# Attention values on one core: leading and trailing parts as one operand of 128 columns, two products per block, halves added by DVE

## The chip, the cores and the metric

The kernel runs on one core of a Trainium2 chip. The metric is the time of one execution in microseconds (us), the median over the runs shown. TensorE is called PE (PEld is its loading of the stationary operand), VectorE DVE, ScalarE ACT, GpSimd POOL, SyncE SP.

## The reference, cut to what matters

One transformer-like layer of 512 frames and 1024 channels: a projection, three mixers (a state space model, an attention, a spatial gating unit), a gated merge, a residual norm, a feed-forward block and a second residual norm, all in float32. The change touches the attention's last step alone. With 8 heads of 64 channels and blocks of 128 queries, it is

```
p = jax.nn.softmax(s, axis=-1).astype(v.dtype)
return jnp.einsum('bhqk,bkhd->bqhd', p, v)
```

where the mask keeps a key when its chunk of 64 frames is not later than the query's, so a block of 128 keys meets the queries from its own block on: 512, 384, 256 and 128 of them for the four key blocks.

## The kernel before

Every float32 operand x of a large product is split into a leading part (x rounded to the type fp32r, by ACT as a rule) and a trailing part (x minus the leading part, by DVE as a rule). A product is made of three: leading by leading, leading by trailing, trailing by leading. `mm3` (line 72) issues these three matmuls into one PSUM bank.

All engines' instructions are put in order when the kernel is built, by a planner (class at line 83, its loop `run` at line 380). Tasks are generators; each holds the next operation, or three matmuls as one group that is not parted. The planner knows a cost for each operation, takes the one that could start first by its own clock, and lets one of lower priority number pass if that would start nearly as soon. So the main stream (priority 5.0) is filled in wherever the attention (2.0) isn't ready; norm and weight tasks (0 to 0.5) go ahead of both, and the dot products of the modulation (`ada2`, 3.0) come behind the attention. On the chip each engine takes its instructions strictly in the planned order and waits on semaphores.

The main stream (`main`, line 1468) is, around the attention: `kept_gates(0)` (tiles `pz`, 24 matmuls each), then `branch(0, ...)` for the state space result (tiles `pp` out of `zs`, 12 matmuls each, eight tiles), then `branch(1, ...)` for the attention's result (tiles `pp` out of `ymla`, eight tiles of 12), the output projection (`po` out of `mT`) and the first norm (`norm1`, line 1847), whose transposed result feeds the feed-forward block. `branch(1, ...)` is planned only when the last head has been planned. Of its first tile, matmuls 10 to 12 are the first to read the last of the four `ymla` tiles.

The attention has one task per head (`head`, line 839). In order: the query product `pq`, scaled and split into `qh` (DVE, ACT, DVE); four score tiles `s`, each with DVE's fill and maximum, ACT's exponential, DVE's reciprocal and ACT's scaling into `pr`; the transposes `px` of `pr` on PE, evicted as leading and trailing parts `pb` (ACT, then DVE) of 512, 384, 256 and 128 columns; for each key block j three matmuls into `po`, with 64 columns of the value tile `vv` as the stationary operand and `pb` moving; ACT's copy of `po` into half the rows of `o`; after every second head the split of `o` into `ymla` (ACT, DVE). A head's transposes and values begin after the values of the head before are done (`o_done`), and its scores after the scores of the head before (`s_done`). PSUM has 8 banks: four are kept for the main stream, so the attention has at most four, three of which (`po` and two `px`) belong to a head's values.

The value tiles are made once, early, in `latents` (line 751): per block of 128 frames one product `pv` of 128x512, ACT's copy to the leading half of the tile, DVE's difference to the trailing half.

Of the kernel before, what the change touches and what calls it, by code (L numbers as in the profile page):

```python
# [14 lines left out]
AF = mybir.ActivationFunctionType  # L15
ALU = mybir.AluOpType
# [3 lines left out]
P = 128  # L20
# [3 lines left out]
NT = 4  # L24
# [43 lines left out]
def ts(i, n=P):  # L68
    return slice(i * n, (i + 1) * n)


def mm3(o, w, x, start, stop):

    T = PE[0]
    return [(T, "matmul", (o, w[0], x[0]), dict(start=start, stop=False)),
            (T, "matmul", (o, w[0], x[1]), dict(start=False, stop=False)),
            (T, "matmul", (o, w[1], x[0]), dict(start=False, stop=stop))]
# [5 lines left out]
class Planner:  # L83
# [27 lines left out]
    class Recorder:  # L111
# [8 lines left out]
        def drop(self, *tiles):  # L120
            self.ops.append((None, self.plan.drop, tiles, {}))
# [103 lines left out]
    def get(self, pool, cls, name, shape=None, dt=F32):  # L225
        yield lambda: self.pools[pool].room(cls)
        return self.take(pool, cls, name, shape, dt)

    def gets(self, pool, cls, *names):

        p = self.pools[pool]
        yield lambda: p.room(cls) if p.free_for(cls) >= len(names) else INF
        return [self.take(pool, cls, n) for n in names]
# [200 lines left out]
def hybrid_kernel(ctx: ExitStack, tc: tile.TileContext, a: dict, out: bass.AP):  # L434
# [6 lines left out]
    V, S, G, T, Y = pl.V, pl.S, pl.G, pl.T, pl.Y  # L441
    get, gets, take, drop, hold, when, spawn = pl.get, pl.gets, pl.take, pl.drop, pl.hold, pl.when, pl.spawn
# [8 lines left out]
    def f(ap):  # L451
        return ap.bitcast(F32)


    def sl(w, s):
        return w[0][:, s], w[1][:, s]
# [259 lines left out]
    L = {}  # L716
# [34 lines left out]
    def latents():  # L751
        r = pl.Recorder(pl)
# [16 lines left out]
        yield from r.run()  # L769
        kvn = L["kvn"]  # L770
        w = yield from wv.wait()
        L["vv"] = []
        for t in range(NT):
            o = yield from get("s4", "x", "vv", (P, 2, N), F32R)
            pv = yield from get("ps", "x", "pv")
            for c in range(2):
                r.mm3(pv, (kvn[c][:, 0, ts(t)], kvn[c][:, 1, ts(t)]), sl(w, ts(c, 512)), c == 0, c == 1)
            r.S.activation(o[:, 0, :], pv, AF.Copy)
            r.V.tensor_tensor(o[:, 1, :], pv, f(o[:, 0, :]), op=ALU.subtract)
            r.drop(pv)  # L780
            yield from r.run()
            L["vv"].append(o)
        wv.free()
        v_done.set()
        yield kv_go
# [7 lines left out]
        for hh in range(2):  # L793
            o = 64 * (1 - hh)
# [9 lines left out]
        for p in range(4):  # L804
# [6 lines left out]
            for e in range(2):  # L811
                q = slice(64 * e, 64 * e + 64)
# [3 lines left out]
            for e in range(2):  # L816
                q = slice(64 - 64 * e, 128 - 64 * e)
# [21 lines left out]
    def head(h):  # L839
        e = h % 2  # L840
        r = pl.Recorder(pl)
# [12 lines left out]
        pq = yield from get("ps", "x", "pq")  # L854
# [38 lines left out]
        for t in (3, 2, 0, 1):  # L893
            n = P * (t + 1)
# [14 lines left out]
        vv = L["vv"]  # L909
        if h > 0:  # L910
            yield o_done[h - 1]
        po, *pxs = yield from gets("ps", "x", "po", "px", "px")
        po = po[:64, :]

        turned = [Event() for _ in range(NT)]

# [19 lines left out]
        for j in range(NT):  # L936
            yield turned[j]
            n = N - P * j
            pb = pt[j, "b"]
            yield mm3(po[:, P * j:], (vv[j][:, 0, ts(h, 64)], vv[j][:, 1, ts(h, 64)]), (pb[:, 0, :n], pb[:, 1, :n]),  # L940
                      j == 0, j == NT - 1)
            drop(pb)
        drop(*(pt[t, "t"] for t in range(1, NT)))
        o = o32[h // 2]
        r.S.activation(o[64 * e:64 * e + 64, :], po, AF.Copy)
        r.drop(po)
        yield from r.run()
        o_done[h].set()
# [4 lines left out]
            yield from r.run()  # L953
        heads_left[0] -= 1
        if heads_left[0] == 0:
            drop(*vv)
            ymla_done.set()

    s_done = [Event() for _ in range(HEADS)]
# [508 lines left out]
    def main():  # L1468
# [17 lines left out]
        for m in range(4):  # L1486
            spawn(put_u(m), POST)
        spawn(latents(), LAT0)
        spawn(ada2(), ADA)
        for h in range(HEADS):  # L1490
            spawn(head(h), ATT + 0.01 * h)
# [491 lines left out]
```

## Time and profile before

| | us |
|---|---|
| median of 3 runs (lowest, highest) | 880.0 (879.49, 880.49) |
| the profiled execution's own time | 878.67 |
| its span | 876.9 |
| PE busy in the span | 852.6 |
| DVE busy | 593.8 |
| ACT busy | 365.0 |
| POOL busy | 88.7 |

The profile is of one execution; the span runs from its first instruction to its last. In the profile every operation carries line 97, the planner's helper, so groups are told apart by tile names. A matmul's own duration holds its passage through the array, which overlaps with the next one's; the distance from one start to the next is what a matmul costs in a stream. The chain of waits shows such costs, since it counts each piece up to the start of the next.

### The profile page before, as it was taken

Reading aid. Unit: us, or ns where it says so; the run is one execution under the profiler, and the core shown is the slowest. Engines: PE = TensorE matmul, PEld = TensorE weight load, DVE = VectorE, ACT = ScalarE, POOL = GpSimd, SP = SyncE. Lnnn points to the kernel's source line nnn. Section 1 sums busy time; section 2 is a strip of 40 time slices with the busy share of each in tenths; the row PEclk is TensorE's granted clock in tenths of the full one; section 3 lists DMA queues with packets and bytes.
Section 4 is the critical chain, followed back from the end, with each engine's and each line's share of the span. In section 5 each row is a group of like instructions: output and inputs, shape, how many; then the busy total and the mean of one; then the engine's idle time right before and its main releaser. Section 6 shows DMA issues by size and latency. Waiting matters only on the chain.

```text
span 876.9 us, 11401 instructions
## 1 busy us (share of the span) xinstructions
PE 852.6 (97%) x4258; PEld 710.0 (81%) x4258; DVE 593.8 (68%) x1161; ACT 365.0 (42%) x614; POOL 88.7 (10%) x98
## 2 busy tenths in 40 slices
PE   9999999999999989999999799999999999999995
PEld 8888888888888868888887699888888888888884
DVE  6989999999977579887859974634433334125436
ACT  3556554555446557675334543122222222211301
POOL 0003113202021000000002500000000000001025
PEclk9999999999999989999999999999999999999998
DMA  9972133434584344676730517322222222322401
GB/s 340 405 264 74 49 108 108 136 107 149 174 291 135 101 178 167 230 255 222 270 121 29 188 60 257 117 76 86 79 73 96 72 79 92 119 96 96 144 25 72
DMA packets 43975, 125.87 MB, mean 144 GB/s; under 512 B 5008, under 2 KB 9616, under 8 KB 43920
## 3 DMA queue, kind: packets, MB, share of 16 engines
q1 hardware_dynamic: 43920, 125.15, 41.0%
q8 instruction: 33, 0.54, 0.2%
q14 instruction: 22, 0.18, 0.1%
HBM read 114.65 MB, written 10.49 MB: 143 GB/s over the span
## 4 chain that ended last, share of the span: by engine, by line
PE 82%; DVE 11%; issue 2%; ACT 2%; DMA 1%; POOL 1%; SPq 0%; DVEq 0%; POOLq 0%; ACTq 0%
PE pfa L97 15%; PE pfo L97 13%; PE pfb L97 11%; PE pz L97 10%; PE pp L97 7%; PE po L97 5%; PE pg L97 4%; PE pus L97 3%; PE pvs L97 3%; PE pq L97 2%; PE pcq L97 2%; DVE gi L97 2%; PE s L97 2%; DVE xres L97 1%; DVE wl L97 1%
## 5 line engine op out<-in xcount | busy, mean ns | idle before, releaser
L97 DVE TENSOR_TENSOR wl<-wr,wh 128x1024 fp32r<-128x1024 f32 (+2 forms) x130 | 156.7, 1220 | 75.9 <-ACT wh L97 67.0
L97 ACT ACTIVATE wh<-wr 128x1024 fp32r<-128x1024 f32 (+1 forms) x137 | 139.5, 1039 | 96.3 <-PE pfo L97 48.2
L97 PE MATMUL pfa<-hT,wh 128*128 128x512 f32 (+1 forms) x544 | 136.0, 342 | 0.0
L97 PE MATMUL pz<-hT,wh 128*128 128x512 f32 x384 | 122.3, 399 | 0.0
L97 PE MATMUL pfo<-wh,gT 128*128 128x512 f32 (+1 forms) x396 | 111.3, 367 | 0.0
L97 PEld LDWEIGHTS pfa<-hT,wh 128*128 128x128 f32 x544 | 93.3, 190 | 13.0
L97 PE MATMUL pfa<-hT,wl 128*128 128x512 f32 (+1 forms) x272 | 92.7, 341 | 0.0
L97 PE MATMUL pfb<-hT,wh 128*128 128x512 f32 x288 | 90.3, 394 | 0.0
L97 PEld LDWEIGHTS pz<-hT,wh 128*128 128x128 f32 x384 | 70.3, 188 | 15.2
L97 PEld LDWEIGHTS pfo<-wh,gT 128*128 128x128 f32 x396 | 71.6, 188 | 12.7
L97 PE MATMUL pz<-hT,wl 128*128 128x512 f32 x192 | 75.9, 395 | 0.2 <-DVE wl L97 0.2
L97 PE MATMUL pfo<-wl,gT 128*128 128x512 f32 (+1 forms) x198 | 72.7, 367 | 0.0
L97 PEld LDWEIGHTS pfb<-hT,wh 128*128 128x128 f32 x288 | 53.9, 187 | 13.3
L97 ACT ACTIVATE gT<-ftg 128x512 fp32r<-128x512 f32 (+1 forms) x26 | 14.7, 566 | 114.4 <-DVE ftg L97 114.4
L97 DVE TENSOR_TENSOR ftg<-ftg,pfb 128x512 f32<-128x512 f32 x18 | 12.4, 687 | 73.3 <-PE pfb L97 73.3
L97 DVE SCALAR_TENSOR_TENSOR ada<-ada,cact 128x1024 f32<-128x1024 f32 x48 | 58.3, 1225 | 0.0
L97 PEld LDWEIGHTS pfa<-hT,wl 128*128 128x128 f32 x272 | 51.5, 189 | 6.7
L97 PE MATMUL pfb<-hT,wl 128*128 128x512 f32 x144 | 56.7, 394 | 0.0
L97 POOL TENSOR_TENSOR wl<-wr,wh 128x1024 fp32r<-128x1024 f32 x7 | 17.7, 2536 | 331.2 <-ACT wh L97 312.2
L97 PEld LDWEIGHTS pz<-hT,wl 128*128 128x128 f32 x192 | 36.0, 187 | 9.4 <-DVE wl L97 0.7
L97 PEld LDWEIGHTS pfo<-wl,gT 128*128 128x128 f32 x198 | 37.3, 188 | 6.3
L97 PE MATMUL po<-wh,mT 128*128 128x512 f32 x128 | 41.0, 394 | 0.0
(270 smaller groups left out, 1496.0 us busy)
## 6 DMA issues: line engine op xcount, KB each, us to landing
wr<-in_w_f SPq DMA_DIRECT2D x66, 512.0 KB, 3.2
ada<-in_w_ada SPq DMA_DIRECT2D x48, 512.0 KB, 6.4
wr<-in_w_gate SPq DMA_DIRECT2D x24, 512.0 KB, 3.6
wr<-in_w_br SPq DMA_DIRECT2D x12, 512.0 KB, 3.6
dg<-tg SPq DMA_DIRECT2D x16, 256.0 KB, 2.1
tg<-dg SPq DMA_DIRECT2D x16, 256.0 KB, 3.7
wr<-in_w_out SPq DMA_DIRECT2D x8, 512.0 KB, 4.0
wr<-in_w_g SPq DMA_DIRECT2D x8, 448.0 KB, 8.7
```

The lines of the kernel that those rows point to most:

```text
L97: r = fn(*a, **kw)
```

## The change

The value tile of a frame block is laid out anew. Before, its 1024 columns were 512 leading and then 512 trailing ones. After, each head has 128 columns side by side: leading, trailing for an even head, trailing, leading for an odd one. ACT and DVE write it through views with runs of 64 and of 128 columns. The stationary operand of a head is now these 128 columns. For each key block there are two matmuls, one with the leading and one with the trailing part of `pb`, and `po` has 128 rows: 64 of the products with the leading values, 64 of those with the trailing ones. So the product of trailing by trailing, left out before, is now included. At a head's end ACT copies the trailing half of `po` to the rows of `o`, across partitions, and DVE adds the leading half from PSUM.

```
--- before.py
+++ after.py
@@ -769,17 +769,21 @@
         yield from r.run()
         kvn = L["kvn"]
         w = yield from wv.wait()
-        L["vv"] = []
+        L["vv"], L["vt"] = [], []
         for t in range(NT):
             o = yield from get("s4", "x", "vv", (P, 2, N), F32R)
             pv = yield from get("ps", "x", "pv")
             for c in range(2):
                 r.mm3(pv, (kvn[c][:, 0, ts(t)], kvn[c][:, 1, ts(t)]), sl(w, ts(c, 512)), c == 0, c == 1)
-            r.S.activation(o[:, 0, :], pv, AF.Copy)
-            r.V.tensor_tensor(o[:, 1, :], pv, f(o[:, 0, :]), op=ALU.subtract)
+
+            q = o.rearrange("p i n -> p (i n)").rearrange("p (a b c) -> p a b c", a=4, b=4)
+            pq = pv.rearrange("p (a b c) -> p a b c", a=4, b=2)
+            r.S.activation(q[:, :, 0:4:3, :], pq, AF.Copy)
+            r.V.tensor_tensor(q[:, :, 1:3, :], pq, f(q[:, :, 0:4:3, :]), op=ALU.subtract)
             r.drop(pv)
             yield from r.run()
-            L["vv"].append(o)
+            L["vv"].append(o.rearrange("p i n -> p (i n)"))
+            L["vt"].append(o)
         wv.free()
         v_done.set()
         yield kv_go
@@ -910,7 +914,6 @@
         if h > 0:
             yield o_done[h - 1]
         po, *pxs = yield from gets("ps", "x", "po", "px", "px")
-        po = po[:64, :]
 
         turned = [Event() for _ in range(NT)]
 
@@ -937,12 +940,15 @@
             yield turned[j]
             n = N - P * j
             pb = pt[j, "b"]
-            yield mm3(po[:, P * j:], (vv[j][:, 0, ts(h, 64)], vv[j][:, 1, ts(h, 64)]), (pb[:, 0, :n], pb[:, 1, :n]),
-                      j == 0, j == NT - 1)
+
+            yield [(T, "matmul", (po[:, P * j:], vv[j][:, ts(h)], pb[:, i, :n]),
+                    dict(start=j == 0 and i == 0, stop=j == NT - 1 and i == 1)) for i in range(2)]
             drop(pb)
         drop(*(pt[t, "t"] for t in range(1, NT)))
         o = o32[h // 2]
-        r.S.activation(o[64 * e:64 * e + 64, :], po, AF.Copy)
+        m, x = slice(64 * e, 64 * e + 64), slice(64 - 64 * e, 128 - 64 * e)
+        r.S.activation(o[m, :], po[x, :], AF.Copy)
+        r.V.tensor_tensor(o[m, :], po[m, :], o[m, :], op=ALU.add)
         r.drop(po)
         yield from r.run()
         o_done[h].set()
@@ -953,7 +959,7 @@
             yield from r.run()
         heads_left[0] -= 1
         if heads_left[0] == 0:
-            drop(*vv)
+            drop(*L["vt"])
             ymla_done.set()
 
     s_done = [Event() for _ in range(HEADS)]
```

## Rows read from the trace of the kernel before

**Rows 1.** The page of the profile: busy time, share and instructions of each engine, and the chain that ended last, by engine.

```profile
PE 852.6 (97%) x4258; PEld 710.0 (81%) x4258; DVE 593.8 (68%) x1161; ACT 365.0 (42%) x614; POOL 88.7 (10%) x98
...
PE 82%; DVE 11%; issue 2%; ACT 2%; DMA 1%; POOL 1%; SPq 0%; DVEq 0%; POOLq 0%; ACTq 0%
```

**Rows 2.** Busy time in stretches through the attention and one behind it: the stretch and its length, then busy time (instructions) of PE, PEld, DVE, ACT, POOL, the granted clock, DMA share and GB/s. The sum is over ten stretches, 319 to 419 us and 450 to 460 us.

```profile
392.00:404.00 12.00, 12.00 (x72) 10.06 (x72) 8.25 (x20) 9.17 (x23) 0.00 (x0) 1.00 0.36 127
404.00:416.00 12.00, 12.00 (x67) 9.88 (x67) 9.04 (x20) 6.04 (x14) 0.00 (x0) 1.00 0.80 280
...
450.00:460.00 10.00, 10.00 (x45) 8.26 (x44) 0.28 (x1) 0.00 (x0) 0.00 (x0) 1.00 0.16 54
sum 110.00, PE 109.97 PEld 90.93 DVE 85.10 ACT 66.00 POOL 0.00; mean PE 11.00 PEld 9.09 DVE 8.51 ACT 6.60 POOL 0.00
```

**Rows 3.** The chain of waits from 380 to 420 us: start, us until the next piece, engine, tile, matmuls.

```profile
385.99 0.69 PE s L97 x3
...
387.59 1.22 PE po L97 x6
...
388.92 0.52 PE s L97 x3
...
390.83 0.69 PE s L97 x6
391.52 0.53 PE po L97 x6
...
400.21 1.56 PE po L97 x9
...
401.88 1.22 PE s L97 x9
...
416.03 4.16 PE pp L97 x18
```

**Rows 4.** The chain of waits from 318 to 345 us, same columns.

```profile
320.78 0.96 PE po L97 x3
...
323.02 0.77 PE po L97 x6
```

**Rows 5.** PE in order of time, the first head's values: start, duration, operation, operands, count, idle before it.

```profile
315.48 0.45 PE L97 MATMUL po<-pb,vv 128*64 128x512 f32 x1 [1.35 <-ACT pb L97]
317.00 1.11 PE L97 MATMUL po<-pb,vv 128*64 128x512 f32 x2 [1.07 <-DVE pb L97]
317.91 0.63 PE L97 MATMUL px<-ident,pr 128*128 128x128 f32 x2
```

**Rows 6.** Stretches around that place, columns as in rows 2.

```profile
320.00:322.00 2.00, 2.00 (x7) 1.41 (x7) 2.00 (x4) 0.00 (x0) 0.00 (x0) 0.50 1.03 420
322.00:324.00 2.00, 2.00 (x11) 1.66 (x10) 0.51 (x2) 0.17 (x1) 0.00 (x0) 0.65 0.77 244
```

**Rows 7.** PE in order of time, a later head's values between other work (columns as in rows 5).

```profile
387.20 0.39 PE L97 MATMUL pp<-zs,wl 128*128 128x512 f32 x1
387.43 1.38 PE L97 MATMUL po<-pb,vv 128*64 128x512 f32 x6
388.65 0.27 PE L97 MATMUL px<-ident,pr 128*128 128x128 f32 x1
```

**Rows 8.** The instructions that write or read the tile `po`, by shape: count, duration in ns (least, median, most), first and last start. The rows with `mT` are the output projection's; `po` is a bank's name in both.

```profile
L97 PEld LDWEIGHTS po<-wh,mT x128: 187/188/190, 440.2 to 488.1; 128*128 128x128 f32 x128
L97 PE MATMUL po<-wh,mT x128: 388/389/481, 440.4 to 488.3; 128*128 128x512 f32 x128
L97 PEld LDWEIGHTS po<-pb,vv x96: 132/134/231, 315.5 to 415.7; 128*64 128x64 f32 x96
```

**Rows 9.** Groups on DVE from 300 to 420 us: operation, tiles, shapes, count, busy us, mean ns, idle before.

```profile
L97 DVE SCALAR_TENSOR_TENSOR ada<-ada,cact 128x1024 f32<-128x1024 f32 x16 | 19.4, 1215 | 0.0
...
L97 DVE SCALAR_TENSOR_TENSOR zs<-s5s,zs 128x512 fp32r<-128x512 f32 x4 | 4.4, 1100 | 5.3 <-ACT zs L97 5.3
...
L97 DVE TENSOR_TENSOR k<-pk,k 64x512 fp32r<-64x512 f32 x2 | 1.4, 684 | 0.7 <-ACT k L97 0.7
```

**Rows 10.** DVE in order of time, from the seventh head's values into the last head (columns as in rows 5).

```profile
400.17 0.41 DVE L97 TENSOR_TENSOR pb<-px,pb 128x256 fp32r<-128x256 f32 x1
...
403.22 1.23 DVE L97 TENSOR_TENSOR wl<-wr,wh 128x1024 fp32r<-128x1024 f32 x1
...
405.07 0.69 DVE L97 TENSOR_TENSOR macc<-macc,tg 128x512 f32<-128x512 f32 x1
...
405.99 0.29 DVE L97 TENSOR_REDUCE mx<-s 128x1 f32<-128x128 f32 x1
...
413.71 0.61 DVE L97 TENSOR_TENSOR pb<-px,pb 128x256 fp32r<-128x256 f32 x2
...
417.35 0.69 DVE L97 TENSOR_TENSOR ymla<-o,ymla 128x512 fp32r<-128x512 f32 x1 [0.39 <-ACT ymla L97]
```

**Rows 11.** ACT in order of time, the copies of `po` of the last two heads.

```profile
404.00 0.59 ACT L97 ACTIVATE o<-po 64x512 f32<-64x512 f32 x1
...
416.06 0.59 ACT L97 ACTIVATE o<-po 64x512 f32<-64x512 f32 x1 [2.32 <-PE po L97]
```

**Rows 12.** The instructions on the tile `vv`, by shape.

```profile
L97 DVE TENSOR_TENSOR vv<-pv,vv x4: 676/682/683, 79.5 to 87.1; 128x512 fp32r<-128x512 f32 x4
```

**Rows 13.** PE in order of time, its longest idle time behind the attention, in the first norm.

```profile
504.75 1.12 PE L97 MATMUL pxt<-ident,xres 128*128 128x128 f32 x4 [5.38 <-DVE xres L97]
```

More of the change, by code (lines that the diff above doesn't have):

```diff
@@ L771, in latents @@
         w = yield from wv.wait()
-        L["vv"] = []
+        L["vv"], L["vt"] = [], []
         for t in range(NT):
@@ L777, in latents @@
                 r.mm3(pv, (kvn[c][:, 0, ts(t)], kvn[c][:, 1, ts(t)]), sl(w, ts(c, 512)), c == 0, c == 1)
-            r.S.activation(o[:, 0, :], pv, AF.Copy)
-            r.V.tensor_tensor(o[:, 1, :], pv, f(o[:, 0, :]), op=ALU.subtract)
+            q = o.rearrange("p i n -> p (i n)").rearrange("p (a b c) -> p a b c", a=4, b=4)
+            pq = pv.rearrange("p (a b c) -> p a b c", a=4, b=2)
+            r.S.activation(q[:, :, 0:4:3, :], pq, AF.Copy)
+            r.V.tensor_tensor(q[:, :, 1:3, :], pq, f(q[:, :, 0:4:3, :]), op=ALU.subtract)
             r.drop(pv)
             yield from r.run()
-            L["vv"].append(o)
+            L["vv"].append(o.rearrange("p i n -> p (i n)"))
+            L["vt"].append(o)
         wv.free()
@@ L912, in head @@
         po, *pxs = yield from gets("ps", "x", "po", "px", "px")
-        po = po[:64, :]
         turned = [Event() for _ in range(NT)]
@@ L939, in head @@
             pb = pt[j, "b"]
-            yield mm3(po[:, P * j:], (vv[j][:, 0, ts(h, 64)], vv[j][:, 1, ts(h, 64)]), (pb[:, 0, :n], pb[:, 1, :n]),
-                      j == 0, j == NT - 1)
+            yield [(T, "matmul", (po[:, P * j:], vv[j][:, ts(h)], pb[:, i, :n]),
+                    dict(start=j == 0 and i == 0, stop=j == NT - 1 and i == 1)) for i in range(2)]
             drop(pb)
@@ L944, in head @@
         o = o32[h // 2]
-        r.S.activation(o[64 * e:64 * e + 64, :], po, AF.Copy)
+        m, x = slice(64 * e, 64 * e + 64), slice(64 - 64 * e, 128 - 64 * e)
+        r.S.activation(o[m, :], po[x, :], AF.Copy)
+        r.V.tensor_tensor(o[m, :], po[m, :], o[m, :], op=ALU.add)
         r.drop(po)
@@ L955, in head @@
         if heads_left[0] == 0:
-            drop(*vv)
+            drop(*L["vt"])
             ymla_done.set()
```

## The prediction

> **What bounds the kernel now.** I read the busy times of the page first, then the chain that ended last, then the busy times by stretch, and last the order of work on PE, DVE and ACT around the attention. The page shows PE busy for 852.6 of 876.9 us and 82% of the chain on PE [rows 1]: PE's own work is the bound almost everywhere. The stretches sharpen that for the place of the change. From 319 to 419 us and from 450 to 460 us PE is busy for 109.97 of 110 us; DVE has 85.10 us, of which 0.28 us lie in the last ten [rows 2], so 84.8 of 100 us in the attention. PE never waits there, since the main stream's groups of three matmuls fill every gap of the heads. But the heads have the better priority, so they advance as fast as their own chain (PE, DVE, ACT and four PSUM banks) lets them, and the filling is what is left over. Two ends must be watched therefore: the end of the filling and the end of the last head. Today they nearly meet: after the last head's last values, at 416.03, come 18 matmuls in 4.16 us [rows 3], of which 12 still belong to the state space branch (12 x 0.231 = 2.8 us) and 6 to the attention's branch. So the filling outlasts PE's work for the heads by 2.8 us.
>
> **PE's part.** 96 products become 64. In the chain a head's twelve take 1.22 + 0.53 = 1.75 us. The score matmuls have the shapes of the new products, 128 stationary columns and 512, 384, 256 and 128 moving ones: three of 512 take 0.69, three of 384 0.52, three of 256 with three of 128 0.69 [rows 3], together 1.90 us. Two thirds of that is 1.27, so a head saves 0.48 us. That is less than a third of 1.75, since the narrow block pays for the wider operand: a load of 128 columns lasts 188 ns, one of 64 134 ns [rows 8]. The first head saves more, because its values run at half the clock: after PE had waited 1.35 and 1.07 us for `pb` [rows 5] the granted clock was 0.50 from 320 to 322 us and 0.65 in the next two [rows 6], the lower of the two levels, 1.2 GHz, for most of the values. It loses one matmul of 512 of about 0.45 us ((317.91 - 317.00) / 2, rows 5), a third of 0.96 = 0.32, and of the 0.77 us for the small blocks [rows 4] some 0.1. Sum: 7 x 0.48 + 0.87 = 4.2 us. The two waits themselves stay: the first new product also needs the leading part of `pb`, the second the trailing one.
>
> **DVE's part.** Eight additions of 64x512 with one operand in PSUM; the nearest row is the difference of 64x512 out of PSUM, 684 ns [rows 9]: 8 x 0.69 = 5.5 us. DVE has 15 us free in the attention's 100 us, and 16 dot products of 1.2 us from 300 to 420 us [rows 9] are work that may come later; from 450 to 460 us DVE is all but idle [rows 2]. So its sum is hidden. Its place is not: the addition stands behind ACT's copy and ahead of the next head's maxima. At the seventh head's end the copy ran at 404.00 [rows 11] and DVE went from a weight difference at 403.22 through 405.07 to the next head's maximum at 405.99 without a pause [rows 10]; there 0.69 us would go straight into the last head's scores. Where DVE has a gap it costs nothing. Against it, PE's values stand in front of scores whose bank is free already: DVE finished the `pb` that frees it at 400.58 [rows 10], nine `po` matmuls ran from 400.21 for 1.56 us, and the scores began at 401.88 [rows 3]; a third less of them gives back up to 0.5 us. So a head's cycle changes by -0.5 to +0.69 us. I take 0: one cost and one gain of nearly one size, each in some of the cycles. The first head's 0.87 us do move all later heads, since the second head's queries stand among them on PE.
>
> **The rest.** ACT copies 64x512 as before. That it crosses partitions I cost at 0, bounds -0.1 to +0.3 us a head, inside the range for the cycle. The value tiles are written through views: 8 instructions near 80 us, now 0.68 us each on DVE [rows 12]. A write that takes every fourth element took 1.10 us for 128x512 [rows 9], so between 0 and 8 x 0.42 = 3.4 us, nearer to 0 as runs of 64 stay whole; the main stream's matmuls cover it, and the first use is 230 us later. Without that cover it would cost those 3.4 us. `po` is held for another 0.7 us; the next head takes it only with its own transposes. No DMA is added or moved past a queue.
>
> **A rule of the skill.** PE went from 128-column matmuls into the 64-column ones and out again at its usual pace: 387.20 to 387.43, then six in 1.22 us until the next tile's 388.65 [rows 7]. The Trainium skill says in TensorEngine Tiling (Array Packing), section Key Properties, that changing the tiling mode drains TensorE; a 64-column stationary operand is such a mode. By the rows the change removes no drain and the sum stays; by the rule it would remove some, which is the fourth rival.
>
> **Sum.** The filling now ends at 418.8 - 4.2 = 414.6 us. The last head ends 0.87 us earlier by the first head's saving, and up to 1.1 us more once no filling stands in front of its last values (DVE began the last two `pb`, 0.61 us together, at 413.71 [rows 10], so they could start at 414.4 and started at 415.5, 0.53 before 416.03 [rows 3]): between 414.1 and 415.2. One wait is new. The attention's branch reads the last `ymla` with its tenth matmul, 9 x 0.23 = 2.1 us after its start. The copy began at 416.06 [rows 11] and that `ymla` was done at 417.35 + 0.69 = 418.04 [rows 10], 2.0 us behind the last values; with the addition it is 2.7. So PE waits up to 0.7 us there, which no filling covers any more. The gain lies between 4.2 - 0.1 = 4.1 us (the last head ends at 414.1, so its `ymla` is there at 416.8, the tenth matmul's turn at 414.6 + 2.1) and 2.8 - 0.7 = 2.1 (the last head doesn't move); at 415.2 it is 418.8 - 415.2 - 0.7 = 2.9. I take 3.0. Behind it, all waits for PE until the first norm, where DVE, free before, starts when PE hands over: the gain is carried through as a shift. The profiled execution took 878.67 us, 1.77 more than its span and 1.33 less than the median of 880.0; 878.67 - 3.0 = 875.7, and on the median's footing 877.0.
>
> **Rivals.** First, the heads' chain is the bound and DVE's additions outweigh PE's relief: each of seven cycles grows by 0.3 us, 2.1 in all; the last head then ends near 416.03 - 0.87 + 2.1 = 417.3, the branch ends its wait 0.7 later at 418.0, against 418.8 before: gain 0.8, time 879.2. For it speaks DVE's load of 9.04 of 12 us in the last cycle with no pause in its middle; against it, 8.25 of 12 in the one before [rows 2].
>
> Second, the slow side: the same place, but every addition lands in front of the next head's maxima and the full 0.69 us goes into each cycle, 4.8 us. The last head ends at 416.03 - 0.87 + 4.8 = 420.0, the branch is free at 420.7: 1.9 us lost. PE, with its filling gone at 414.6, idles for some 5 us; the first head's two waits of 2.4 us together were followed by about 5.5 us at half clock [rows 5, 6], which would cost another 2.7. Time 881.9 to 884.6, say 883.3. It decides from a growth of 0.4 us a cycle ((418.8 - 0.7 - 415.2) / 7), where nothing is gained.
>
> Third, the order is planned anew from the first values on, so other pairs may collide. In the first norm PE idled for 5.38 us before one transpose [rows 13]; half of that either way is what another order there could do. It widens the range and isn't a forecast.
>
> Fourth, the drains: each head's values stand in two groups on PE, so 8 x 2 x 2 = 32 changes; a matmul's 389 ns [rows 8] less its distance of 0.23 us bounds one at 0.16 us, 5.1 us in all, and the time would be 871.9. The rows show none.
>
> Last, the change might not shorten PE at all, if the two products' loads bound them. The scores, which load as much, stand against it.
>
> **Chances.** Of changes within 0.2% (1.8 us) a measurement of this kernel can tell nothing. Forecast 0.50, by itself 875.5 to 878.2; first rival 0.26; second 0.21, with the third's bad orders; drains 0.03, with its good ones. Faster: forecast and drains, 0.53. Same: 0.26. Slower: 0.21. The range for 8 in 10 goes from 874.0, better than the forecast by the third rival's luck, to 882.8, close to the second rival's middle.
>
> **What would show it.** PE: 64 `po` products from `vv`, a head's eight in 1.27 us of the chain; else the first term is wrong. DVE: eight additions of about 0.69 us. The first `pp` out of `ymla` near 415 us instead of 418.8; idle time of PE before it names the first two rivals, and a clock below 1 there the second. From 450 us on, the order of before, some 3 us earlier; if the attention ends earlier and the end doesn't, the first norm is where to look. The prediction is wrong if a head's cycle grows by more than 0.4 us.

## The result, and the profile after

The changed kernel takes 884.87 us, the median of 4 runs (883.66 to 885.42), against 879.79 us (879.49 to 880.49, 4 runs) of the kernel before beside it: a ratio of 1.0059, 95% interval 1.0044 to 1.0074. The prediction was 877.0 us and its range ended at 882.8. The change is slower, and by more than the range allowed for.

The profiled execution took 885.05 us with a span of 883.3 us, 6.4 us longer in either than that of before. Its page, busy time by engine:

```profile
PE 853.8 (97%) x4226; PEld 712.9 (81%) x4226; DVE 597.8 (68%) x1167; ACT 365.7 (41%) x612; POOL 95.3 (11%) x102
```

PE lost 32 instructions [rows 1], as it should: 96 products became 64. Yet its busy time rose by 1.2 us: more of it ran at the lower clock (the mean granted clock of the span is 0.986, before 0.990), and PE now waits. The new order also moves work between engines: without the additions DVE and ACT have two instructions fewer each and POOL has four more; pe_only below also has four more there and is not slower. The stretches of the attention (columns as in rows 2) say where:

```profile
392.00:404.00 12.00, 12.00 (x61) 10.09 (x60) 11.15 (x26) 6.38 (x16) 1.24 (x2) 1.00 0.31 105
404.00:416.00 12.00, 7.92 (x46) 6.45 (x45) 11.44 (x27) 6.08 (x13) 0.00 (x0) 0.99 0.69 232
320.00:420.00 100.00, 95.37 (x483) 80.11 (x482) 86.62 (x197) 63.40 (x142) 6.00 (x4) 0.97 0.62 213
```

From 404 to 416 us PE is busy for 7.92 of 12 us, where it was busy throughout [rows 2]. DVE has 11.15 and 11.44 of 12 us in the two stretches, where it had 8.25 and 9.04. Two additions of 0.69 us lie in those 24 us (396.73 and 414.19), so 1.4 us of the 5.3 that DVE has more there are additions; the rest is other work that stands there now.

ACT's copies of `po` mark the heads' ends (start, duration, operation, idle before). Before:

```profile
323.83 0.59 ACT L97 ACTIVATE o<-po 64x512 f32<-64x512 f32 x1 [3.93 <-PE po L97]
341.85 0.59 ACT L97 ACTIVATE o<-po 64x512 f32<-64x512 f32 x1
...
392.22 0.59 ACT L97 ACTIVATE o<-po 64x512 f32<-64x512 f32 x1
```

The last two stand in [rows 11]. After:

```profile
323.07 0.59 ACT L97 ACTIVATE o<-po 64x512 f32<-64x512 f32 x1 [3.59 <-PE po L97]
346.45 0.59 ACT L97 ACTIVATE o<-po 64x512 f32<-64x512 f32 x1
...
394.47 0.59 ACT L97 ACTIVATE o<-po 64x512 f32<-64x512 f32 x1 [1.64 <-PE po L97]
413.56 0.59 ACT L97 ACTIVATE o<-po 64x512 f32<-64x512 f32 x1
422.95 0.59 ACT L97 ACTIVATE o<-po 64x512 f32<-64x512 f32 x1 [0.94 <-PE po L97]
```

The first head ends 0.76 us earlier; 0.41 of that lie ahead of its first product already (315.07 against 315.48 [rows 5]). The second takes 23.38 us in place of 18.02 and the seventh 19.09 in place of 11.78; the other cycles together are shorter. The last head ends at 422.95, 6.9 us late. The chain of waits shows what stood in the seventh cycle and behind it:

```profile
400.57 4.76 PE pp L97 x21
...
406.57 0.98 ACT pb L97 x2
407.55 0.96 ACT wh L97
...
409.67 0.69 DVE tg L97
...
410.39 0.69 DVE macc L97
411.08 0.80 DVE pb L97 x2
...
421.70 1.23 PE po L97 x8
```

PE runs 21 filling matmuls in one piece ahead of the seventh head's transposes and soon after has none left; then its next step hangs on ACT's split of a weight, and on DVE's `tg` and `macc`, which belong to the main stream and stand ahead of the head's `pb`; and behind them on `modc`, rows for the adaptive scales. The last line is a piece that the prediction asked for: a head's eight products in 1.23 us. PE's own line for `modc` has the wait in brackets:

```profile
415.97 2.50 PE L97 MATMUL pc<-ident,modc 128*128 128x128 f32 x10 [2.59 <-DVE modc L97]
```

The output projection is the first work that no head can delay any more. In the two chains it begins here, before and after:

```profile
440.59 19.82 PE po L97 x87
```

```profile
445.50 19.82 PE po L97 x87
```

So 4.9 of the 6.4 us are lost ahead of it, and the rest behind it; by the medians the change costs 5.1 us. I use the projection's start below as the measure of the attention, beside the time of the whole kernel. A trace is of one execution: in the seven traces that keep the old order up to there (the kernel before and six runs below) the first head's first product starts anywhere from 314.93 to 316.07 us. Differences of about 1 us between two traces therefore say nothing.

### The profile page after: what moved, and what is told of

Its sections match the earlier page's. It is cut to its first block, busy times and chain, and to the rows that moved or that the text cites. A ratio compares the mean times of both kernels' runs of the same rounds, so it can differ in the third digit from the quotient of the medians.

```text
span 883.3 us, 11340 instructions
## 1 busy us (share of the span) xinstructions
PE 853.8 (97%) x4226; PEld 712.9 (81%) x4226; DVE 597.8 (68%) x1167; ACT 365.7 (41%) x612; POOL 95.3 (11%) x102
## 4 chain that ended last, share of the span: by engine, by line
PE 83%; DVE 11%; issue 2%; ACT 2%; DMA 1%; POOL 1%; SPq 0%; POOLq 0%; ACTq 0%; DVEq 0%
PE pfa L97 16%; PE pfo L97 13%; PE pfb L97 11%; PE pz L97 11%; PE pp L97 7%; PE po L97 4%; PE pg L97 4%; PE pus L97 3%; PE pvs L97 3%; PE pcq L97 2%; PE pq L97 2%; DVE xres L97 1%; DVE gi L97 1%; PE s L97 1%; PE py L97 1%
## 5 line engine op out<-in xcount | busy, mean ns | idle before, releaser
L97 DVE TENSOR_TENSOR wl<-wr,wh 128x1024 fp32r<-128x1024 f32 (+1 forms) x128 | 154.5, 1222 | 73.5 <-ACT wh L97 64.8
L97 ACT ACTIVATE wh<-wr 128x1024 fp32r<-128x1024 f32 (+2 forms) x137 | 139.5, 1039 | 98.2 <-PE pfo L97 48.2
L97 PE MATMUL pfa<-hT,wh 128*128 128x512 f32 (+1 forms) x544 | 138.0, 345 | 0.0
L97 POOL TENSOR_TENSOR wl<-wr,wh 128x1024 fp32r<-128x1024 f32 (+1 forms) x9 | 22.5, 2499 | 429.5 <-ACT wh L97 313.8
```

What stands on the lines that cost most here:

```text
L97: r = fn(*a, **kw)
```

## The experiments

Two theories stood at first. *Order*: every engine's order is planned from estimated costs, the new costs gave another order, and that order is worse. *Additions*: DVE's eight additions stretch the chain from head to head, as the second rival had it. The first experiments therefore keep the order of before and change the work alone. The planner is told the old cost of the products, and the addition is put in behind ACT's copy without being counted:

```
             if ins[0].dtype == F32R:
+            if outs[0].tensor.name in self.pos:
+                return 1.5 * (max(size(ins[1]) / 2400.0, 0.1067 / 2) + 0.0135), False
...
-        r.V.tensor_tensor(o[m, :], po[m, :], o[m, :], op=ALU.add)
+        r.call(pl.issue, (V, "tensor_tensor", (o[m, :], po[m, :], o[m, :]), dict(op=ALU.add)))
```

**both_old_order**, all the work in the old order:

> All the work of the change, but the planner counts a head's values as it did before (two products at the cost of the old three, the addition at none), so every engine keeps the order of the kernel before and the additions are put in right behind ACT's copies. Theory order (the loss is the new order: the third head's query weights are loaded 6 us later and ACT, DVE and then PE wait for them; PE's part itself gains): 876 to 879.5 us. Theory additions (DVE's eight additions stretch the heads' chain in any order): 882 to 887 us.

**pe_old_order**, the same without the addition; it copies the leading half only:

> Two products of 128 columns, without the additions (only the leading half of the values goes on, the trailing half is left out), in the order of the kernel before. Both theories: PE's 4.2 us come out but for what the heads' chain keeps, 875.5 to 878 us. If it stays at 880, PE's work was never the bound in this stretch and the first term of the prediction is wrong.

**add_old_order**, the kernel before with an operation of the addition's shape at the addition's place:

> The kernel before with its three products, and eight DVE operations of 64x512 on po and its copy (a maximum of equal values) at the place of the additions, in the order of the kernel before. Theory order: DVE's free time takes most of it, 880 to 882 us. Theory additions: 5 us or more lost, 885 to 888 us.

**pe_only**, two products and no addition, planned anew:

> Two products of 128 columns, without the additions (only the leading half of the values goes on, the trailing half is left out), planned anew. Theory additions: the loss is gone, 875 to 878 us. Theory order: any new order can collide, so the time may lie on either side of pe_old_order by some us, and it is above 878 us if orders planned anew are worse as such.

Measured, with the ratio to the kernel before and its interval: both_old_order 881.32 us (1.0019, 1.0006 to 1.0033), pe_old_order 877.45 (0.998, 0.997 to 0.9989), add_old_order 884.15 (1.0052, 1.0035 to 1.0068), pe_only 878.03 (0.9984, 0.9975 to 0.9994). The projection's start in the first three, in that order:

```profile
444.26 19.82 PE po L97 x87
```

```profile
437.54 19.82 PE po L97 x87
```

```profile
443.96 19.81 PE po L97 x87
```

The products alone bring it forward by 3.05 us, the additions alone put it back by 3.4, and both together by 3.7. The last number is of an execution of 883.43 us, where the median of seven is 881.32. By the medians the products save 2.8 us beside the additions too (884.15 to 881.32), so this trace doesn't show that the additions swallow their saving. Both theories hold a part: the additions cost some 4 us on top of the products in the old order (881.32 against 877.45), and the changed kernel is slower still, 884.87.

**Is it DVE's work or its wait?** In both_old_order DVE stands idle before each of the eight additions. DVE's waits from 318 to 425 us (what waited, on what, us in total, times, longest):

```profile
DVE o L97 <- ACT o L97: 3.8, 8, 1.0
DVE pb L97 <- ACT pb L97: 2.8, 5, 1.0
DVE ada L97 <- DMA ada<-in_w_ada: 1.7, 1, 1.7
```

**work_old_order** puts DVE work of the same size at the same place, tied to nothing:

```
         r.S.activation(o[64 * e:64 * e + 64, :], po, AF.Copy)
+        scr = sb.tile([P, 1], F32, tag="mx", name="scr", bufs=8)
+        h64 = slice(64 * e, 64 * e + 64)
+        r.call(pl.issue, (V, "tensor_reduce", (scr[h64, :], f(hT[0][h64, 0, :])), dict(op=ALU.max, axis=AX.X)))
```

> The kernel before with its order kept on every engine, and eight more DVE reductions (64 partitions x 512, out of SBUF into a scratch column that nobody reads) exactly where the additions stand behind ACT's copy of a head's values; nothing waits for them and they wait for nothing. Each is expected near 0.69 us. add_old_order, with the same amount of DVE work at the same place but bound to ACT's copy and ahead of the ymla split, came out at 884.15, 4.8 above before, and DVE stood 3.8 us in all waiting for that copy. If DVE's own 5.5 us of work is what stretches the heads' chain, this comes out at 883 to 884.5. If it is the wait for ACT's copy, with everything queued behind it, this comes out at 879.4 to 881. In between (882) both carry it in like parts.

Measured 880.88 us (1.0017, 1.0006 to 1.0029), the projection at 441.98; the eight took as long as the additions:

```profile
L97 DVE TENSOR_REDUCE scr<-hT x8: 658/678/684, 322.9 to 417.6; 64x1 f32<-64x512 f32 x8
```

So 5.5 us of DVE's work by itself costs some 1.4 us of time, and being tied between ACT's copy and the pair's split costs another 3.3 (884.15 in add_old_order). The reduction reads SBUF and holds no bank, so the 3.3 us stand for all that ties the addition down: the copy ahead of it, the split behind it, and the bank of `po`, which it keeps longer. Two later runs tried to get those 3.3 back by moving the tied steps out of the way, with nothing else moved. **both_later4** lets four of the eight additions stand four or five instructions later on DVE; **both_all_later** moves three more, by one to four, and the splits of three pairs three or four instructions later on ACT.

> both_old_order (881.32) with the additions of the first, third, fifth and seventh head four instructions later on DVE and nothing else moved; the other four stay right behind ACT's copy, since the split needs them. In both_old_order DVE waited 1.01, 0.52, 0.46 and 0.19 us for ACT's copy ahead of these four, 2.2 of 3.8 us in all. If the wait is the larger part of the additions' price, this comes out 1 to 2.2 us lower, at 879.1 to 880.3, and the output projection begins near 442.5 in place of 444.3. If it is DVE's work, wherever it stands, no change: 881 to 882.

> both_later4 (882.04) with one more thing moved: the split of a pair's values (ymla) stands two instructions later on ACT, and the addition of the second, fourth and sixth head one instruction later on DVE, so that ACT no longer waits for the addition (0.76 us each, 2.3 in all for these three, in both_old_order) with the next head's exponentials behind it. The last head stays as it is. If that wait is the rest of the additions' price, this comes out at 879.5 to 880.5, and the output projection begins near 442. If the price is DVE's 5.5 us in a chain that is full, 881 to 882 again.

Both missed: 882.04 us (1.0023, 1.001 to 1.0036) and 884.32 (1.0052, 1.0038 to 1.0066), the latter 3.0 us above both_old_order. DVE's waits in both_later4 show why:

```profile
DVE pb L97 <- ACT pb L97: 3.0, 5, 1.0
DVE ada L97 <- DMA ada<-in_w_ada: 2.4, 1, 2.4
DVE o L97 <- ACT o L97: 1.6, 4, 0.5
...
DVE q L97 <- PE pq L97: 1.5, 1, 1.5
```

The wait for ACT's copy fell by 2.2 us as intended, and 2.4 us came back before `q`, `ada` and `pb`. The Trainium skill calls ACT, DVE and GpSimd strict FIFOs (Perfetto Trace Analysis, section Tensor Engine Instruction (MATMUL, LD_WEIGHTS)); the traces agree, since DVE's other 1161 instructions stand in the same order in both, and DVE, early at one place, only waited for the next producer. In both_all_later DVE stands 2.2 us before the last step of the moved splits instead. Which tie makes the 3.3 us stays open; neither of the two waits that were moved makes them by itself.

**Which of the new costs gives the bad order?**

> The kernel before with three products, and one DVE operation of 64x512 per head behind ACT's copy (a maximum of the values and their copy, which leaves them as they are), in the order that the planner makes when it counts these operations. The same work in the old order took 884.15. If planning anew is what makes the changed kernel slower than both_old_order (881.32 against 884.87, 3.5 us), this comes out above 885, at some 886 to 888. If the planner puts counted additions well and the new order's loss comes from the cheaper products, this comes out at or below 884, at 881 to 884.

> All the work of the change, planned with the cost of two products but without the additions, which are put in right behind ACT's copies: the order of pe_only (878.03) and the additions of both_old_order. If the additions' cost is the same 4 us in any order that doesn't count them, this is 878.0 + 3.9 = 881.9. If the new order's loss comes from the products' new cost, it is near the changed kernel, 884 to 885.5; if it comes from the planner counting the additions, it is at 881 to 882.5.

> All the work of the change, planned with the additions counted but with the two products counted as the three of before. If counting the additions is what makes the new order bad (later weight loads and adaptive rows, as in the changed kernel), this is at 884 to 886. If the products' new cost does it, this is at 881 to 882. If neither alone does, both this and both_pe_order are near 881.5 and the loss of the changed kernel belongs to the one order that its costs happen to give.

Measured: add_only 881.64 us (1.002, 1.001 to 1.003), both_pe_order 880.71 (1.0009, 1.0 to 1.0019), both_add_order 879.91 (1.0004, 0.9995 to 1.0014). Neither cost alone does it; counting the additions alone even helps, since add_only is 2.5 us below add_old_order, the same work in the old order. The work of the change runs at 879.9 to 881.3 us in these three orders and at 884.9 in its own, so the changed kernel's loss beyond 880 to 881 belongs to the one order that both costs together happen to give. It isn't the only bad one: both_all_later above (884.32) and add_low below (883.53) do the same work too.

**A suspect in that order that was cleared.** In the changed kernel ACT waited 3.60 us for the third head's query weights, whose load stood on SP behind a store that waits for its tile. In the three others it stood ahead. **load_first** swaps these two neighbours, which go out at 326.91 (store) and 327.32 us (load) in the changed kernel. SP after the swap (start, duration; the planner's helper has lines 102 and 105 in this run and the next):

```profile
323.38 0.39 SPq L105 DMA_DIRECT2D wr<-in_w_q  x1
327.01 0.33 SPq L102 DMA_DIRECT2D dg<-tg  x1
```

> The changed kernel with two neighbours swapped on SP and nothing else on any engine: the load of the third and fourth heads' query weights stands ahead of the store of one gate tile (dg<-tg) in place of behind it. In the changed kernel that store waits for its tile until 326.91 us, the load goes out at 327.32, ACT waits 3.60 us for it, and the second head ends 4.6 us later than before; in the three other orders of the same work (881.3, 880.7, 879.9) the load goes out at 320.8 to 323.9. If this queueing is what sets the changed kernel's order apart, this comes out at 880 to 881.5, with the second head's end near 342 and the output projection near 441.5. If the loss belongs to other parts of that order (PE's 2.59 us for the adaptive rows and 1.50 us for pb near 410), it stays at 884 to 885.

> The opposite swap in both_add_order (879.91): the same store of a gate tile ahead of the same load of query weights on SP, nothing else. If the queueing is the cause, the load goes out near 328, the second head ends 3 to 5 us later, and the time is 882.5 to 884.5. If the filling and the later heads take it up, it stays at 879.5 to 880.5, and the changed kernel's loss needs the rest of its order too.

load_first took 884.31 us (1.006, 1.0045 to 1.0075), load_late, the opposite swap in both_add_order, 881.09 (1.0019, 1.0009 to 1.0029), between its two forecasts, its interval overlapping that of its parent. The split of that load on ACT, in the changed kernel, in load_first and in load_late:

```profile
331.00 0.84 ACT L97 ACTIVATE wh<-wr 128x768 fp32r<-128x768 f32 x1 [3.60 <-DMA wr<-in_w_q]
```

```profile
327.47 0.86 ACT L105 ACTIVATE wh<-wr 128x768 fp32r<-128x768 f32 x1
```

```profile
329.61 0.85 ACT L105 ACTIVATE wh<-wr 128x768 fp32r<-128x768 f32 x1 [3.74 <-DMA wr<-in_w_q]
```

In load_first the load went out at 323.38 us instead of 327.32, the wait was gone, and nothing followed: the second head ended at 346.55 and the projection began at 445.52. In load_late the wait came, and the second head ended at 343.19 us, against 343.29 in both_add_order. The theory fell. A wait of 3.6 us on ACT lay beside a chain that was late for other reasons.

**Is it the order alone, whatever work runs in it?** **before_new_order** runs the old work in exactly the changed kernel's order: the planner counts two products and an addition, which is then not issued.

```
+        if method == "tensor_tensor" and a[1].tensor.name in self.pos:
+            self.issued(e, method, a, kw)
+            return
...
+            if outs[0].tensor.name in self.pos:
+                return (max(size(ins[1]) / 2400.0, 0.1067) + 0.0135) * 2 / 3, False
```

> The work of the kernel before (three products, no addition, the values laid out as before) in exactly the order that the changed kernel has on every engine: the planner is told the cost of two products and of an addition which isn't issued. If the order by itself is what costs 3 to 4 us, this comes out at 882.5 to 884.5, with PE idle near 410 for the adaptive rows as in the changed kernel. If the order costs only together with the additions on DVE, this is near before, 879 to 880.5. If the order is good for the old work, below 879.

> Two products per block in exactly the changed kernel's order on every engine, without the additions (leading half only; the planner counts an addition that isn't issued). The old work in this order took 886.5, the whole change in it 884.87. If the products give their 4.2 us where PE's filling no longer covers the heads, this is 886.5 - 4.2 = 882.3 and the additions cost 2.6 in this order. If the order's gaps swallow the additions, this is 884 to 885, and the products give 1.5 to 2. If the additions cost here what they cost in the old order (4 us), 880.5 to 881.

before_new_order took 886.5 us (1.0081, 1.0064 to 1.0098): the new order costs the old work some 7 us. **pe_new_order**, the changed kernel without its additions, took 883.5 (1.0045, 1.0031 to 1.006). With the runs of the old order this fills a table of work against order, each as its difference from the kernel before:

| work | old order | new order |
|---|---|---|
| three products (before) | 0 | +0.81% |
| two products, no addition | -0.20% | +0.45% |
| two products and additions | +0.19% | +0.59% |
| three products and eight operations like the additions | +0.52% | not run |

Each row is one work, each column one order. In the old order the products gain 0.20%, or 0.33% beside the additions, and the additions cost 0.39 to 0.52%. In the new order the products gain 0.36% (3.2 us) and the additions cost 0.14% (1.2 us, within the two intervals). So the work of the change is a gain of 0.22% where the new order already lets PE wait (the intervals overlap a little, but all four times with it, up to 885.42 us, lie below all four without, from 886.24), and a loss of 0.19% where it doesn't; the order costs between 0.4 and 0.8%. Most of that lies in the attention: the projection of before_new_order starts 5.9 us later than before, of 7.8 us between the two traces.

```profile
446.53 19.81 PE po L97 x87
```

Stretches and heads' ends of before_new_order, without any addition, have the changed kernel's marks:

```profile
392.00:404.00 12.00, 12.00 (x64) 9.93 (x63) 9.68 (x25) 6.40 (x16) 1.24 (x2) 1.00 0.30 102
404.00:416.00 12.00, 9.65 (x55) 7.74 (x53) 11.60 (x24) 4.95 (x11) 0.00 (x0) 1.00 0.62 211
```

```profile
322.96 0.59 ACT L97 ACTIVATE o<-po 64x512 f32<-64x512 f32 x1 [3.49 <-PE po L97]
346.32 0.59 ACT L97 ACTIVATE o<-po 64x512 f32<-64x512 f32 x1
...
395.75 0.59 ACT L97 ACTIVATE o<-po 64x512 f32<-64x512 f32 x1 [1.99 <-PE po L97]
414.97 0.59 ACT L97 ACTIVATE o<-po 64x512 f32<-64x512 f32 x1 [0.16 <-PE po L97]
```

The second head takes 23.36 us and the seventh 19.22, as in the changed kernel to 0.15 us, PE idles from 404 to 416 us, and DVE is full there with 11.60 of 12. In pe_new_order, also without additions, PE is busy for 8.15 of these 12 us. So the gap doesn't come from the additions. That the pile of DVE's other work at that place is what holds the seventh head is what the chain reads; no run moved it alone.

**Versions that might beat both.** All have the change's whole work, planned anew. **add_low** makes the additions tasks of lower priority, **pool_new_order** lets ACT copy both halves and POOL add them, **pair_add** lets ACT copy both halves and DVE add once for a pair of heads, and **pair_add_old_cost** is the latter planned with the old cost of the products:

```
-        r.V.tensor_tensor(o[m, :], po[m, :], o[m, :], op=ALU.add)
+        r.S.activation(o2[h // 2][m, :], po[m, :], AF.Copy)
...
+            r.V.tensor_tensor(o, o, o2[h // 2], op=ALU.add)
             r.split(o, *pair(ymla[h // 2]))
```

> All the work of the change, planned anew, with the additions as a task of their own at lower priority (the last head's excepted): the next head no longer waits for the addition, only for ACT's copy, and the split of an odd head's values waits for both additions. If the additions' price lies in their place between ACT's copy and the next head's maxima, this comes out at 876.5 to 879, as pe_only (878.0) with the additions hidden. If DVE's 5.5 us of work is the price wherever it stands, 880 to 882. If what decides is the order that happens to come out, anything from 878 to 885.

> All the work of the change, planned anew, but the halves are added by POOL out of two copies by ACT, so DVE has nothing of it. It adds eight ACT copies of 64x512 (0.59 us each, 4.7 us, where ACT idles over half of the time) and eight POOL additions of 64x512, estimated at 1.3 us each from POOL's 2.5 us for 128x1024. A head's end is then some 1.2 us later than with DVE's addition, but DVE's queue isn't held up. If DVE's work and its wait are the price, this comes out at 877.5 to 879.5, near pe_only (878.0). If the length of the way from a head's last values to its end is the price, it is slower than both_old_order, 882 to 885.

> All the work of the change, planned anew, with one addition for two heads: ACT copies both halves of each head's values (eight more copies of 64x512, 0.59 us each), and DVE adds 128x512 once ahead of the odd head's split (four times 0.69 in place of eight). The next head waits for ACT's two copies alone and never for DVE. If DVE's wait and work between heads is the price of the change (4 us on both orders that could be compared), this comes out at 877.5 to 879.5. If the second copy on ACT costs as much as the addition did, 880 to 882. If its order comes out as badly as the changed kernel's, 883 to 886, and then the split by its twin tells.

> The same work as pair_add, planned with the two products counted as the three of before (as both_add_order, 879.91, was). If the additions' place is the price, this and pair_add both lie at 877.5 to 879.5. If plan decides more than place, the two differ by 2 us or more, as the changed kernel and both_add_order do by 5.

All are slower than the kernel before: add_low 883.53 us (1.0047, 1.0032 to 1.0062), pool_new_order 886.4 (1.008, 1.0065 to 1.0095), pair_add 892.15 (1.0143, 1.0128 to 1.0158), pair_add_old_cost 888.68 (1.0104, 1.0089 to 1.0119). pair_add lies 6 us above the worst that was expected of it; its twin differs from it in the planned order alone, by 3.5 us. Halving DVE's additions helped in neither order. A reading that no run tested: the second copy occupies a buffer from one head to its partner's end, so the next probabilities are late. PE's waits in pair_add:

```profile
PE px L97 <- ACT pr L97: 5.9, 3, 3.6
PE px L97 <- DVE pb L97: 3.0, 4, 1.3
```

The best version with the whole work, both_add_order, can't be told from the kernel before.

## Why the prediction was wrong, point by point

*What bounds the kernel now* was read rightly: PE's filling covers the heads, and two ends nearly meet. What the change does to that balance was misjudged: from 320 to 420 us PE is busy for all of 100 us before, for 99.8 in pe_old_order, for 98.5 in add_old_order, and for 95.4 in the changed kernel and in pe_new_order.

*PE's part* held in a stream: a head's eight products take 1.23 us (predicted 1.27). With the order kept, the products alone moved the projection by 3.05 us (predicted 3.0) in one trace each, but the time by 1.9 us (interval 1.0 to 2.6); the last section names a place behind the attention where the two traces differ by 0.9. The first head's 0.87 us did not come out. From its first product to ACT's copy it takes 8.35 us before and 8.00 in the changed kernel, but over all traces the median is 7.92 us with three products (five traces, 7.89 to 8.35) and 7.99 with two (fifteen, 7.31 to 8.01). The products of 384 did take 0.32 us less; what the first block saved went into the next wait. The third transpose behind it, before and after:

```profile
319.03 0.47 PE L97 MATMUL px<-ident,pr 128*128 128x128 f32 x1 [0.48 <-DVE pb L97]
```

```profile
318.61 0.47 PE L97 MATMUL px<-ident,pr 128*128 128x128 f32 x1 [0.85 <-DVE pb L97]
```

It starts 3.55 us behind the first product before and 3.54 after, since it waits for DVE's `pb` either way. The prediction kept the first two waits and left out this third one.

*DVE's part* failed in its place, not its size. The additions took 689 ns each as predicted:

```profile
L97 DVE TENSOR_TENSOR o<-po,o x8: 676/689/697, 323.7 to 423.6; 64x512 f32<-64x512 f32 x8
```

"So its sum is hidden" is the first wrong step: even untied, DVE's 5.5 us cost 1.4 us (work_old_order). "I take 0" for a head's cycle is the second. From the first to the last head's end it takes 416.06 - 323.83 = 92.23 us before, 413.01 - 323.15 = 89.86 in pe_old_order, 419.44 - 323.30 = 96.14 in add_old_order and 419.73 - 322.31 = 97.42 in both_old_order. Over seven cycles the products alone take 0.34 us off each, the additions alone add 0.56, and both together add 0.74, where the prediction had -0.5 to +0.69. The trace of both_old_order lies 2.1 us above the median of that kernel, so 0.74 is rather too much. Still, gain and cost did not cancel: by the medians the additions cost 3.9 us on top of the products (877.45 to 881.32). The step counted the instruction and its place ahead of the maxima; it left out that DVE waits for ACT's copy ahead of it, and ACT for the addition ahead of the split. Being tied costs 3.3 us, through which of the ties is open.

*The rest* held: the strided writes of the values take 683 to 685 ns on DVE, against 676 to 683 [rows 12], and ACT's copy across partitions 591 to 596 ns.

*The rule of the skill.* By the rule on drains in TensorEngine Tiling (Array Packing), section Key Properties, of the Trainium skill, a kernel without 64-column products would have come out near 871.9 us, the fourth rival's time; pe_old_order, where only the additions are missing, took 877.45. So a drain of the size that the fourth rival allowed isn't there, as the rows had it. The page gives no time, and the runs can't exclude a much shorter one.

*Rivals.* The first and second named the right mechanism in the old order; 881.32 us lies between their 879.2 and 883.3. The second's test, a cycle that grows by more than 0.4 us, was met: 0.74 in both_old_order, and 1.09 in the changed kernel (422.95 - 323.07 = 99.88 us). That the changed kernel's 884.87 lies beside the second rival's slow end of 884.6 is luck, since 3.5 us of it are the order's. The third rival was set aside as "isn't a forecast", with half of 5.38 us either way in the first norm. That is the third wrong step, and it cost as much as the additions: the order planned anew loses 3.5 us with the change's work and 7 us with the old, and it does so mostly inside the attention, not in the norm. The sum against the kernel before is then -0.20% for the products, +0.39% for the additions and +0.40% for the order, which makes the measured +0.59%. The prediction priced each piece in the order of before, although the change gives the planner new costs for 64 products and eight additions; the order that follows is part of the change.

## What to carry to other kernels

Where a program plans the order from costs, an edit changes two things; run the new work in the old order and the old work in the new one before either is credited. In this kernel DVE, busy for 85% of the attention, had no room for eight short instructions that wait for one engine and are waited for by another: ask who waits on both sides of an instruction, not only how long it runs. And a long wait in the trace is a suspect only; the longest one on ACT, 3.6 us, was worth nothing when it was taken away.

## What the runs showed of the hardware that was not expected

The loss behind the output projection (1.5 of the 6.4 us) lies at one place, and it is a matter of the clock. After the first norm's wait (5.38 us before [rows 13]) PE restarts at the lower level, 1.2 GHz. The same 318 matmuls, before and after (start, us until the next piece):

```profile
505.87 4.35 PE pfa L97 x30
510.66 36.00 PE pfa L97 x288
546.65 5.60 PE pfb L97 x24
```

```profile
510.77 5.35 PE pfa L97 x30
516.55 36.56 PE pfa L97 x288
553.11 5.60 PE pfb L97 x24
```

From the first to the third line it is 40.78 us before and 42.34 after, 1.6 us more for the same work. In pe_old_order it was 41.72, so 0.9 us of the products' gain went there, and in add_only 40.65. The granted clock from 508 to 514 us of the changed kernel is 0.50, and 0.84 in the two us behind:

```profile
512.00:514.00 2.00, 2.00 (x12) 0.50 0.00 0
514.00:516.00 2.00, 2.00 (x16) 0.84 0.00 0
```

Before, it is 0.58 and 0.57 from 504 to 508 us and 1.00 from there on. The first of these matmuls start at 505.87 there and at 510.77 after the change, so they run at the lower clock for a shorter time:

```profile
506.00:508.00 2.00, 2.00 (x12) 2.00 (x11) 1.82 (x3) 1.18 (x4) 0.00 (x0) 0.57 0.00 0
```

The Trainium skill says in TensorE: Matmul & The Clock Gate, section What's actually happening, that the number of matmuls at the lower clock before the engine is fast again differs from run to run of one kernel. There is one trace of each kernel here, so they agree without proving it: in all twenty, this piece takes 40.65 to 42.79 us, and the kernel before has the second shortest. So a part of the 1.5 us may be chance, and a difference of that size between two single traces with such a restart says nothing about a change. POOL's addition of 64x512 took 1256 to 1973 ns (median 1292) in pool_new_order, where DVE takes 689.
